# One core, a four-part edit of a decoder trunk: the last norm's column chunks, two orders of transfers, and one weight tile's place

## The chip, the cores and the metric

One core of one Trainium2 chip runs the whole program. The metric is the device time of one execution in microseconds (us), taken as the median of several runs. One execution is also profiled: its span is the time from its first to its last recorded instruction, and its own device time stands beside the span.

## The reference

The kernel computes one inference step of a decoder trunk with two layers, in float32, for a prompt of 1024 tokens and for 8 decode tokens (one for each of 8 sequences), with a model width of 1024 (D) and a feed-forward width of 2816 (D_FF). Layer A is a gated linear recurrence (HGRN2, 8 heads of 128). Layer B is sliding-window attention (window 128, 16 query heads of 64, 4 key/value heads) with sinks and a relative-position bias; its keys and values are projected once, after layer A. Each layer is followed by a SwiGLU feed-forward network, and a final RMSNorm gives the output. Cut to the lines that matter:

```python
# every sub-layer: h = h + gate(c) * F(rmsnorm(h) * (1 + scale(c)) + shift(c))
for l in range(2):
    xn = modulate(h, norm_w[l, 0], sh1, sc1)
    if l == 0:   # A: HGRN2 recurrence over chunks of 64, output gate, w_o
        mix, s_new = hgrn2_mixer(xn, w_in_a[l], w_o_a[l], gnorm_a[l], lbs[l], s0, chunk)
    else:        # B: window attention on the shared K/V; decode tokens use the caches
        q = xn @ w_q_b[0]
        att = swa_prompt(q, k_sh, v_sh, sinks, rel_bias)   # or swa_sample(q, k_buf, v_buf, ...)
        mix = att @ w_o_b[0]
    h = h + g1 * mix
    h = h + g2 * swiglu(modulate(h, norm_w[l, 1], sh2, sc2), w_ffn_in[l], w_ffn_out[l])
    if l == 0:   # shared K/V, and the caches moved on by one row
        k_sh, v_sh = split(modulate(h, kv_norm_w, sh_kv, sc_kv) @ w_kv)
        k_state = concatenate([k_buf, k_sh])[:, -WINDOW:]      # same for v
y = rms_norm(h, final_norm_w)
```

## The kernel before

**Data and products.** Activations stand transposed: 128 features on the partitions, tokens along the free axis, 1032 columns (1024 of the prompt, then 8 of decode). Every float32 product is made of three reduced-precision ones: weights and activations are split in a high and a low part, and `mm3` (lines 291 to 293) issues high x high, high x low and low x high into one accumulator. The 1032 columns are cut into equal chunks by a `Grid`: `G3` has 3 chunks of 344 columns, `G4` has 4 of 258. The decode columns are the last 8 of the last chunk (`Grid.last`).

**Weights.** The class `Stream` (object `ws`) holds the order in which weight tiles are used. A unit is loaded by the sync engine's queue (SP; lines 197, 219 and 243) into one of three `raw` buffers, cast by ScalarE (line 182) to the high part, and subtracted by GpSimd, at some places VectorE (line 185), to the low part, in one of 8 `wu` buffers. `ws.next()` hands out the unit that is used now and asks for as many units ahead as fit into `ws.look` buffers, 6 of the 8; a unit of two tiles has size 2, so three such units are ahead.

**Who orders the work.** The program is written as generators (`q_proj`, `wo_first`, `attention` and so on). `run((gen, weight), ...)` takes a step of each in turn, `queue` puts steps behind the current loop, and a `yield` ends a step. A planner then fixes the order of instructions on each engine from their readiness and their order in the program; `fix` and `keep_in_program_order` pin an instruction to its place in the program. The queues themselves run in order: a transfer that waits holds up all that stand behind it on SP.

**The four places.**
1. *Layer A's output projection.* `hgrn_proj(hh)` (line 966) makes the four input projections of head hh with `ws.next()` for each. After the last head, `wo_first` (line 1377) makes the first half of the output projection with four units of W_o, in chunks of `G4`; `wo_product` (line 1369) is one tile of 128 output features by one chunk, 12 matmuls, and `residual` (line 845) adds the gated result to the residual.
2. *The bias tiles.* `biases()` (line 1296) is called once, from the first feed-forward network (`ffn`, line 1599), between two hidden tiles (`seven_products(j)`, some 20 us each): it loads constants, makes a row of 384 biases for each of 16 heads by one matmul and one VectorE addition, writes it to DRAM (`rd`), spreads it to 128 partitions in DRAM (`gd`, 3 MB), loads the sinks and, for each of the 8 decode sequences, one sink column and two pieces of the row, and copies the two caches from DRAM to DRAM.
3. *Layer B's output projection.* Its residual comes back from DRAM (`reload_stack`, line 1425, which issues at line 658): chunk 0 before `next(second)`, chunks 1 to 3 after `next(dec)`. Each chunk is two transfers. `decode_attention` (line 1763) begins with eight transfers, in its first step: the old cache rows (line 1769, four transfers of 128 rows) and the new ones (line 1774, four short ones); its second step transposes them on TensorE (line 1789). `dec_first` runs the rest of it before the projection's last chunk.
4. *The last stage.* The second feed-forward network's last output products run over `G3` chunks and 8 tiles of features (lines 1628 to 1645) with `Final` (line 1994) as their norm. `Final.square` squares the new residual, `then(c)` sums the squares by matmuls with a vector of ones (line 2062), takes the root on VectorE (`newton`, line 542), transposes blocks of 128 tokens back (line 2021), scales the rows and writes them (lines 2040 to 2046). The chunks hold token blocks 0 and 1, 2 to 4, 5 to 7; the last block group's transposes are partly made ahead (`early`, `before_last`), and the decode tokens' rows come with the last chunk:

```python
            if c == LAST:
                dec = [self.turn(NB, lambda k: hd[:, k, :], i, (mmp, axp)[i]) for i in range(2)]
```

## Time and profile before

| | |
|---|---|
| median of 3 runs | 2501.37 us (2498.51, 2501.37, 2503.21) |
| the profiled execution's own time | 2500.0 us |
| its span | 2498.1 us |
| mean granted TensorE clock | 0.996 of full speed |
| busy share of TensorE, VectorE, ScalarE, GpSimd | 98%, 56%, 36%, 31% |
| moved by DMA | 293.43 MB, mean 117 GB/s |

The profile comes from one execution. Busy time of an engine counts its computing instructions; waits, branches and the issue of transfers are not counted. The granted clock is given as a share of full speed: 1.0 is 2.4 GHz, 0.5 is 1.2 GHz. The two rows below the time are of that one execution; the median is of others.

### The profile page before, as it was taken

To read this page: it belongs to the slowest core of one execution; us is meant where nothing else is said; L and a number is where in the kernel's file an instruction comes from. 1 tells how busy PE (TensorE), PEld (TensorE's weight loads), DVE (VectorE), ACT (ScalarE), POOL (GpSimd) and SP (SyncE) were. 2 spreads that over 40 slices of the span, in tenths; PEclk is the share of its full clock that TensorE was granted. 3 is DMA by queue.
4 is the path that set the end of the run, shared out by engine and by line. 5 is a ranking of instruction groups with operands and counts; after the bars stand their busy time and mean duration, and the time that the engine had idled before them with its cause. 6 is when DMAs were issued, how large, how long until landed. Compare 5 with 4: busy or idle time off the path is not lost.

```text
span 2498.1 us, 52373 instructions
## 1 busy us (share of the span) xinstructions
PE 2454.3 (98%) x21557; PEld 2338.0 (94%) x21557; DVE 1390.8 (56%) x3177; ACT 903.0 (36%) x2012; POOL 774.6 (31%) x560
## 2 busy tenths in 40 slices
PE   7999999999999999999999999999999999999998
PEld 5999999998889999999999998878999999999998
DVE  6444444456486554656433735576885555565436
ACT  5333333332363332333211555454643333333112
POOL 1211111111225444544432131002364444445221
PEclk9999999999999999999999999999999999999999
DMA  9465522246833224326321322523222222264101
GB/s 332 146 214 178 170 76 72 70 131 211 267 106 94 82 84 144 97 83 233 123 77 51 93 56 65 165 85 110 69 86 77 77 77 81 82 228 148 65 26 69
DMA packets 314561, 293.43 MB, mean 117 GB/s; under 512 B 28681, under 2 KB 291738, under 8 KB 314290
## 3 DMA queue, kind: packets, MB, share of 16 engines
q1 hardware_dynamic: 313920, 289.86, 35.8%
q8 instruction: 170, 2.79, 0.5%
q14 instruction: 69, 0.57, 0.1%
q10 hardware_dynamic: 402, 0.22, 0.0%
HBM read 231.27 MB, written 63.99 MB: 118 GB/s over the span
## 4 chain that ended last, share of the span: by engine, by line
PE 89%; DVE 4%; DMA 3%; issue 2%; ACT 1%; SPq 0%; POOL 0%; ACTq 0%; DVEq 0%; POOLq 0%
PE mm L291 20%; PE mm L293 19%; PE mm L292 19%; PE ax L291 6%; PE ax L292 6%; PE ax L293 6%; PE ax L470 2%; PE ax L1943 1%; PE ax L1872 1%; PE ax L1098 1%; PE ax L1929 1%; PE ax L1225 1%; PE ax L1188 1%; DMA raw<-in_w_ffn_in_dram 1%; DMA gd<-rd 1%
## 5 line engine op out<-in xcount | busy, mean ns | idle before, releaser
L185 POOL TENSOR_TENSOR wu<-raw,wu 128x512 fp32r<-128x512 f32 x460 | 628.5, 1374 | 1380.1 <-ACT wu L182 1279.4
L291 PE MATMUL mm<-c,wu 128*128 128x344 f32 (+1 forms) x2104 | 673.8, 320 | 2.8 <-ACT c L917 1.7
L293 PE MATMUL mm<-c,wu 128*128 128x344 f32 (+1 forms) x2104 | 660.6, 314 | 1.9 <-issue 1.9
L292 PE MATMUL mm<-c,wu 128*128 128x344 f32 (+1 forms) x2104 | 662.0, 315 | 0.3 <-DVE c L920 0.3
L182 ACT CAST wu<-raw 128x512 fp32r<-128x512 f32 x464 | 286.0, 620 | 665.8 <-PE mm L293 358.5
L291 PEld LDWEIGHTS mm<-c,wu 128*128 128x128 f32 x2104 | 397.4, 189 | 16.1 <-issue 9.4
L292 PEld LDWEIGHTS mm<-c,wu 128*128 128x128 f32 x2104 | 397.8, 189 | 4.2 <-issue 2.6
L293 PEld LDWEIGHTS mm<-c,wu 128*128 128x128 f32 x2104 | 397.9, 189 | 1.8 <-issue 1.8
L291 PE MATMUL mm<-xq,wu 128*128 128x258 f32 x1376 | 390.3, 284 | 2.4 <-ACT wu L182 1.0
L293 PE MATMUL mm<-xq,wu 128*128 128x258 f32 x1376 | 389.6, 283 | 1.3 <-POOL wu L185 1.3
L292 PE MATMUL mm<-xq,wu 128*128 128x258 f32 x1376 | 388.2, 282 | 1.2 <-DVE xq L838 1.2
L291 PE MATMUL ax<-xq,wu 128*128 128x258 f32 x1120 | 316.4, 282 | 0.0
L293 PE MATMUL ax<-xq,wu 128*128 128x258 f32 x1120 | 315.8, 282 | 0.0
L292 PE MATMUL ax<-xq,wu 128*128 128x258 f32 x1120 | 315.6, 282 | 0.0
L291 PEld LDWEIGHTS mm<-xq,wu 128*128 128x128 f32 x1376 | 259.6, 189 | 4.1 <-DVE c L1502 1.2
L292 PEld LDWEIGHTS mm<-xq,wu 128*128 128x128 f32 x1376 | 260.7, 189 | 1.7 <-DVE xq L838 1.7
L293 PEld LDWEIGHTS mm<-xq,wu 128*128 128x128 f32 x1376 | 259.7, 189 | 2.8 <-POOL wu L185 1.5
L845 DVE SCALAR_TENSOR_TENSOR hs<-mm,ada,hs 128x344 f32<-128x344 f32 (+3 forms) x228 | 120.7, 533 | 173.3 <-PE mm L293 164.4
L292 PEld LDWEIGHTS ax<-xq,wu 128*128 128x128 f32 x1120 | 212.1, 189 | 0.0
L291 PEld LDWEIGHTS ax<-xq,wu 128*128 128x128 f32 x1120 | 211.5, 189 | 0.0
L293 PEld LDWEIGHTS ax<-xq,wu 128*128 128x128 f32 x1120 | 211.1, 188 | 0.0
L845 DVE SCALAR_TENSOR_TENSOR c<-mm,ada,c 128x344 f32<-128x344 f32 (+1 forms) x132 | 74.8, 571 | 112.1 <-PE mm L293 111.4
(329 smaller groups left out, 3603.1 us busy)
## 6 DMA issues: line engine op xcount, KB each, us to landing
c<-in_w_ada_dram SPq DMA_DIRECT2D x96, 512.0 KB
raw<-in_w_ffn_in_dram SPq DMA_DIRECT2D x160, 256.0 KB
ff<-c SPq DMA_DIRECT2D x44, 516.0 KB
c<-ff SPq DMA_DIRECT2D x44, 516.0 KB
raw<-in_w_ffn_out_dram SPq DMA_DIRECT2D x44, 512.0 KB
raw<-in_w_in_a_dram SPq DMA_DIRECT2D x32, 512.0 KB
hs<-hs SPq DMA_DIRECT2D x16, 516.0 KB
out_dram<-c SPq DMA_DIRECT2D x16, 512.0 KB
```

Source lines behind the costliest of these rows:

```text
L182: i = act.copy(u[:, 0, :], src)
L185: j = eng.tensor_tensor(u[:, 1, :], src, u[:, 0, :], op=ALU.subtract)
L291: put(pe.matmul(ps, wh, xh, start=first, stop=False))
L292: put(pe.matmul(ps, wh, xl, start=False, stop=False))
L293: put(pe.matmul(ps, wl, xh, start=False, stop=last))
L470: pe.matmul(ada_ps[q][32 * j : 32 * j + 32, 256 * i : 256 * i + 256], cT[:, k, :], u[i][:, j, :], start=(k == 0 and i == 0), stop=(k == KT ...
L845: dve.scalar_tensor_tensor(hc, ps[:, : g.pl[c]], ada[:, gate + n, 0:1], hc, op0=ALU.mult, op1=ALU.add)
L1098: pe.matmul(ps[32 * j : 32 * j + 32, c * 32 : (c + 1) * 32], KS[:, t0 : t0 + 32], QP[:, t0 : t0 + 32], start=True, stop=True, tile_positio ...
L1188: pe.matmul(ps[:, j * P : (j + 1) * P], kt[:, s], vt[:, s], start=True, stop=True)
L1225: pe.matmul(o, attT[:, c, :], vt[:, s], start=(c == 0), stop=True)
L1872: pe.matmul(psv[hf][:, gi, s0:256], q[2 * gp + gi][r, tb * P : (tb + 1) * P], kT[a][r, (tb - 1) * P + s0 : (tb + 1) * P], start=True, stop ...
L1929: pe.transpose(ps[:, g * P : (g + 1) * P], L[:, g, sb * P : (sb + 1) * P], ident)
```

## The change

It has four parts.

1. A class `Blocks` (object `GB`) takes the place of `G3` in the last stage: its chunks are of whole token blocks, (5 to 7 with the 8 decode columns: 392 columns), (2 to 4: 384), (0 and 1: 256), in this order. The decode columns go with the first chunk instead of the last, and so do their residual, squares, scale, sums, root and output rows. Each square now lies in a temporary tile of its own size (`big`) and is added by VectorE or GpSimd in turn; the last one is summed by TensorE straight from its tile, with two blocks instead of three. `wo_product` and `residual` ask the grid for the width of a chunk.
2. `biases()` becomes a generator that is stepped once per hidden tile from the middle one on: constants; the small matmul and the addition; the row's write; the spread with the sinks and the first two of the 8 groups; three times two more groups, the last of them with nothing behind it until the next step; the cache copies. The two row pieces of each group are now pinned.
3. `reload_stack` is stepped in three: chunk 0, chunk 1, chunks 2 and 3. In layer B's projection chunk 1 now comes before `decode_attention`'s first step, which only loads the old cache rows, then come chunks 2 and 3, then its second step with the new rows. In layer A's both reloads run through as before.
4. For the last unit of the last head, `ws.look` is 4 instead of 6, so the third unit of W_o is asked for by the next `ws.next()`, the first of `wo_first`.

```diff
@@ -44,6 +44,9 @@
         self.last, self.nq = self.n - 1, w // Q
+    def width(self, c):
+        return self.w
     def all(self, c):
@@ -51,7 +54,29 @@
         return slice(self.cs[c], self.cs[c] + self.pl[c])
+class Blocks:
+    n, last = 3, 0
+    blocks = ((5, 8), (2, 5), (0, 2))
+    def __init__(self):
+        self.cs = [b0 * P for b0, _ in self.blocks]
+        self.pl = [(b1 - b0) * P for b0, b1 in self.blocks]
+        self.w = max(self.pl) + NB
+    def width(self, c):
+        return self.pl[c] + (NB if c == self.last else 0)
+    def all(self, c):
+        return slice(self.cs[c], self.cs[c] + self.width(c))
+    def prompt(self, c):
+        return slice(self.cs[c], self.cs[c] + self.pl[c])
 G3, G4 = Grid(344), Grid(258)
+GB = Blocks()
 W, NCH, LAST = G3.w, G3.n, G3.last
@@ -846,7 +871,7 @@
         if c == g.last:
-            dve.tensor_tensor(tdec[:, n, :], ps[:, g.pl[c] : g.w], ada[:, gate + n, 1:9], op=ALU.mult)
+            dve.tensor_tensor(tdec[:, n, :], ps[:, g.pl[c] : g.width(c)], ada[:, gate + n, 1:9], op=ALU.mult)
     def residual_dec(tdec):
@@ -968,7 +993,10 @@
         for i in range(4):
+            ws.look = 4 if hh == NH - 1 and i == 3 else RING - 2
             u = ws.next()
+            ws.look = RING - 2
             t = f if i == 0 else big()
@@ -1302,13 +1330,16 @@
         sp.dma_start(outs, k_outside)
+        yield
         ps = axp()
...
         gd = dp.tile([16, P, 384], F32, name="gd")
+        yield
         sp.dma_start(rd, rrow)
+        yield
         sp.dma_start(gd, bc(rd, 1, P))
@@ -1317,13 +1348,16 @@
             fix(sp.dma_start(skd[16 * b : 16 * b + 16, :], sinks_b[0].unsqueeze(1)))
-            sp.dma_start(biasd[16 * b : 16 * b + 16, 1:P], rd[:, P : 2 * P - 1])
-            sp.dma_start(biasd[16 * b : 16 * b + 16, 0:1], rd[:, 2 * P - 1 : 2 * P])
+            fix(sp.dma_start(biasd[16 * b : 16 * b + 16, 1:P], rd[:, P : 2 * P - 1]))
+            fix(sp.dma_start(biasd[16 * b : 16 * b + 16, 0:1], rd[:, 2 * P - 1 : 2 * P]))
+            if b % 2:
+                yield
         fix(sp.dma_start(ck_sample[:, 0 : WIN - 1], cache_swa_k[:, 1:WIN]))
...
             tc.keep_in_program_order(dve.tensor_scalar(t, t, -1.0, None, op0=ALU.mult))
-        return late, biasd, gd, sk, skd
+        yield
+        bs.extend((late, biasd, gd, sk, skd))
     for hh in range(NH):
@@ -1371,7 +1405,7 @@
             xh, xl = o.at(k, g, c)
-            mm3(ps[:, : g.w], wcol(u, 0, i), wcol(u, 1, i), xh, xl, k == 0, k == 3)
+            mm3(ps[:, : g.width(c)], wcol(u, 0, i), wcol(u, 1, i), xh, xl, k == 0, k == 3)
         residual(ps, c, n, gate, tdec, g)
@@ -1426,9 +1460,9 @@
         res.append(st)
-        st.move(src, [0], True)
-        yield
-        st.move(src, range(1, g.n), True)
+        for cs in ([0], [1], range(2, g.n)):
+            st.move(src, cs, True)
+            yield
     def factors(x, st):
@@ -1597,7 +1631,7 @@
         for j in range(PLAIN, NF):
-            if j == NF // 2 and aside:
+            if j >= NF // 2 and aside:
                 aside()
@@ -1630,16 +1664,18 @@
                     last.before_last()
-                wo_product(us[n // 2], o, c, n, gff, tdec, bank=anyp)
+                wo_product(us[n // 2], o, c, n, gff, tdec, last.g, anyp)
                 last.square(c, n)
...
                     last.early()
-            if c == LAST:
+            if c == last.g.last:
                 residual_dec(tdec)
                 last.square_dec()
+            if c == LAST:
                 last.scale_end()
+            if c == last.g.last:
                 last.scale_dec()
@@ -1685,7 +1721,8 @@
     bs = []
-    nkv = ffn(0, X, st, back[0], ToKV, lambda: bs.extend(biases()))
+    bias_steps = biases()
+    nkv = ffn(0, X, st, back[0], ToKV, lambda: next(bias_steps, None))
     late, biasd, gd, nsk, nskd = bs
@@ -1768,6 +1805,7 @@
                 dst.append(t)
+        yield
         for dst, c0 in ((kst, 0), (vst, 256)):
@@ -1975,10 +2013,12 @@
     next(second)
+    next(loads)
     dec = decode_attention()
...
         pass
+    next(dec)
     def dec_first(o=o):
@@ -1992,6 +2032,9 @@
     class Final(Norm):
+        def __init__(self):
+            Norm.__init__(self, GB)
         def scale(self, c, k):
@@ -2000,19 +2043,25 @@
         def scale_tile(self, c, k):
-            s = G3.prompt(c)
+            s = GB.prompt(c)
             return dve.tensor_scalar(h[k][:, s], h[k][:, s], nT[:, 40 + k : 41 + k], None, op0=ALU.mult)
...
         def square(self, c, k):
-            if c < LAST or k < KT - 1:
-                Norm.square(self, c, k)
+            s, n = GB.prompt(c), GB.pl[c]
+            dst = self.acc[k % 2][:, s]
+            if k < 2:
+                act.activation(dst, h[k][:, s], AF.Square)
+                return
+            t = big(cols=3 * P)[:, :n]
+            act.activation(t, h[k][:, s], AF.Square)
+            if c == LAST and k == KT - 1:
+                self.end = t
             else:
-                e0 = G3.prompt(c).start - 5 * P
-                act.activation(self.end[:, e0:], h[k][:, G3.prompt(c)], AF.Square)
+                eng = dve if k % 2 else pool
+                eng.tensor_tensor(dst, dst, t, op=ALU.add)
         def turn(self, parts, src, half, bank, ps=None, ks=range(4), put=lambda i: i):
@@ -2027,12 +2076,10 @@
             flush()
-            self.ahead = {(b, 0): self.block(b, 0, axp) for b in (5, 6, 7)}
-            self.end = big(cols=3 * P)
-            pool.memset(self.end[:, : G3.prompt(LAST).start - 5 * P], 0.0)
+            self.ahead = {(b, 0): self.block(b, 0, axp) for b in range(*GB.blocks[LAST])}
         def before_last(self):
-            for b in (5, 6, 7):
+            for b in range(*GB.blocks[LAST]):
                 self.ahead[b, 1] = self.block(b, 1, mmp, ks=range(2))
@@ -2047,7 +2094,7 @@
             yield LAG
-            b0, b1 = ((0, 2), (2, 5), (5, 8))[c]
+            b0, b1 = GB.blocks[c]
             n = b1 - b0
@@ -2060,25 +2107,23 @@
                 fix(pe.matmul(dst, src, ones[:, 0:1], start=(i == 0), stop=(i == len(sums) - 1)))
+            if c == GB.last:
+                psd = axp()
+                for i, a in enumerate(self.acc):
+                    pe.matmul(psd[:NB, 0:1], a[:, T:TOK], ones[:, 0:1], start=(i == 0), stop=(i == 1))
             if c == LAST:
-                psd = mmp()
-                for i, a in enumerate(self.acc):
-                    fix(pe.matmul(psd[:NB, 0:1], a[:, T:TOK], ones[:, 0:1], start=(i == 0), stop=(i == 1)))
-            if c == LAST:
-                for b in (5, 6, 7):
+                for b in range(b0, b1):
                     self.block(b, 1, None, ps=self.ahead[b, 1], ks=range(2, 4), put=fix)
...
             y = small([P, 12], "ny")
-            if c == LAST:
+            if c == GB.last:
                 dve.memset(ms[:, n : n + 1], 1.0)
...
             dve.tensor_scalar(ms[:, :n], ps[:, :n], 1.0 / D, EPS, op0=ALU.mult, op1=ALU.add)
-            w = n + (c == LAST)
+            w = n + (c == GB.last)
             newton(y[:, :w], ms[:, :w], w, P, "n")
-            if c == LAST:
-                dec = [self.turn(NB, lambda k: hd[:, k, :], i, (mmp, axp)[i]) for i in range(2)]
             yield 1
@@ -2088,7 +2133,8 @@
                 yield 1
-            if c == LAST:
+            if c == GB.last:
+                dec = [self.turn(NB, lambda k: hd[:, k, :], i, axp) for i in range(2)]
                 self.rows(NB, dec, y[:NB, n : n + 1], y_sample.rearrange("b s f -> (b s) f"))
```

## Rows read from the trace of the kernel before

**Rows 1.** The page: busy time, share of the span and instructions of each engine, and TensorE's granted clock in 40 equal slices of the span (9 is 90% or more).

```profile
PE 2454.3 (98%) x21557; PEld 2338.0 (94%) x21557; DVE 1390.8 (56%) x3177; ACT 903.0 (36%) x2012; POOL 774.6 (31%) x560
...
PEclk9999999999999999999999999999999999999999
```

**Rows 2.** Windows of 100 us. Columns: window, its length, busy us (instructions) of PE, PEld, DVE, ACT and POOL, granted clock, DMA share, GB/s.

```profile
500.00:600.00 100.00, 93.54 (x1382) 85.41 (x1380) 58.11 (x138) 31.90 (x101) 10.91 (x8) 0.98 0.58 182
900.00:1000.00 100.00, 97.71 (x805) 96.53 (x804) 52.59 (x103) 28.00 (x57) 43.37 (x32) 1.00 0.37 119
1600.00:1700.00 100.00, 99.16 (x749) 78.62 (x747) 68.31 (x285) 52.39 (x183) 2.58 (x2) 0.98 0.41 129
1900.00:2000.00 100.00, 100.00 (x837) 100.00 (x836) 55.36 (x110) 32.06 (x65) 44.88 (x35) 1.00 0.25 80
2300.00:2400.00 100.00, 100.00 (x638) 100.00 (x637) 42.50 (x78) 16.06 (x23) 31.94 (x21) 1.00 0.20 65
2400.00:2500.00 100.00, 89.07 (x600) 88.15 (x598) 51.34 (x139) 21.11 (x40) 16.89 (x16) 0.97 0.13 49
```

**Rows 3.** Timeline of SP's queue around the bias tiles. Columns: start, length of the group, queue, line, operation, out<-in, count.

```profile
909.37 3.85 SPq L243 DMA_DIRECT2D raw<-in_w_ffn_in_dram  x4
...
936.09 1.47 SPq L1311 DMA_DIRECT2D rd<-c  x1
939.44 0.60 SPq L1312 DMA_DIRECT2D gd<-rd  x1
...
947.75 0.98 SPq L1321 DMA_DIRECT2D late<-rd  x1
952.47 0.32 SPq L1319 DMA_DIRECT2D skd<-in_sinks_b_dram  x1
...
963.01 1.30 SPq L243 DMA_DIRECT2D raw<-in_w_ffn_in_dram  x2
```

**Rows 4.** Timeline of TensorE, some of the instructions that waited. In brackets: the idle time before, and what ended it.

```profile
551.27 0.95 PE L1267 MATMUL ax<-ident,c 128*128 128x128 f32 x4 [2.12 <-DVE c L1254]
...
978.41 0.39 PE L291 MATMUL mm<-xq,wu 128*128 128x258 f32 x1 [0.98 <-ACT wu L182]
...
980.22 0.39 PE L293 MATMUL mm<-xq,wu 128*128 128x258 f32 x1 [1.31 <-POOL wu L185]
...
1627.23 1.06 PE L1789 MATMUL ax<-late,c 128*128 128x8 f32 x8 [0.31 <-ACT c L1785]
...
1629.88 0.42 PE L291 MATMUL mm<-c,wu 128*128 128x258 f32 x1 [0.36 <-DVE hs L845]
```

**Rows 5.** Timeline of SP's queue around layer B's first output projection.

```profile
1611.87 2.45 SPq L1769 DMA_DIRECT2D c<-in_cache_swa_k_dram  x2
1614.38 3.51 SPq L1769 DMA_DIRECT2D c<-in_cache_swa_v_dram  x2
1620.64 4.54 SPq L1774 DMA_DIRECT2D c<-nd  x4
1625.23 4.09 SPq L658 DMA_DIRECT2D hs<-hsc  x6
```

**Rows 6.** The waits of VectorE on transfers between 1600 and 1660: total, times, longest.

```profile
DVE hs L845 <- DMA hs<-hsc: 8.1, 1, 8.1
```

**Rows 7.** Short windows with columns as in rows 2: five us behind the wait at 551, four us from 1630, and one us of the end.

```profile
551.00:556.00 5.00, 4.73 (x27) 4.73 (x28) 3.61 (x9) 0.00 (x0) 0.00 (x0) 0.66 0.99 328
...
1630.00:1634.00 4.00, 4.00 (x21) 4.00 (x22) 2.30 (x11) 0.66 (x4) 0.00 (x0) 0.57 1.09 351
...
2492.00:2493.00 1.00, 0.00 (x0) 0.00 (x0) 1.00 (x2) 0.72 (x2) 0.00 (x0) 1.00 1.01 410
```

**Rows 8.** Timeline of GpSimd and VectorE around the third and fourth unit of W_o.

```profile
528.71 1.29 POOL L185 TENSOR_TENSOR wu<-raw,wu 128x512 fp32r<-128x512 f32 x1 [10.65 <-ACT wu L182]
...
546.13 0.16 DVE L550 TENSOR_TENSOR ot<-ot,oms 128x10 f32<-128x10 f32 x1
...
547.49 2.98 POOL L185 TENSOR_TENSOR wu<-raw,wu 128x512 fp32r<-128x512 f32 x2 [15.29 <-ACT wu L182]
...
547.62 1.28 DVE L550 TENSOR_TENSOR ot<-ot,oms 128x10 f32<-128x10 f32 x1
```

**Rows 9.** Timeline of the end of the program, engines in the order of time.

```profile
2465.64 1.40 PE L2062 MATMUL ax<-ones,c 128*128 128x1 f32 x12
...
2484.78 0.32 PE L293 MATMUL mm<-c,wu 128*128 128x344 f32 x1
...
2485.74 0.48 ACT L2015 ACTIVATE c<-c 128x336 f32<-128x336 f32 x1 [2.17 <-DVE c L845]
...
2487.14 0.16 DVE L2077 TENSOR_SCALAR nms<-ax 128x3 f32<-128x3 f32 x1 [1.10 <-PE ax L2062]
...
2488.09 0.17 DVE L542 TENSOR_SCALAR nt<-nms 128x4 int32<-128x4 int32 x1
...
2488.53 0.60 PE L2021 MATMUL mm<-ident,hd 128*8 128x128 f32 x4
...
2490.34 2.07 DVE L2043 TENSOR_SCALAR c<-mm,ny 128x512 f32<-128x512 f32 x3
...
2491.16 2.85 SPq L2046 DMA_DIRECT2D out_dram<-c  x4
```

## The prediction

> **What bounds the kernel now.** Read the page first: TensorE is busy 98% of the span, no other engine more than 56%, and its clock is at the upper level (2.4 GHz) in nearly every slice [rows 1]. So only two things can shorten the run: less TensorE work, or one of the few places where TensorE stands still or runs at the lower level. The windows of 100 us say where those are [rows 2]: between 1900 and 2000 TensorE is busy for all 100.00 us, but 500 to 600 lacks 6.46 us, 900 to 1000 lacks 2.29, 1600 to 1700 lacks 0.84, and 2400 to 2500 holds the end of the program. The timeline names the instruction that came late at each [rows 4], and for the ones that waited for data the sync engine's queue (SP) says why [rows 3, 5]. All four places lie next to something that the change edits. The sum is made against the profiled execution's own 2500.0 us (span 2498.1), which is 1.4 below the median of the three runs shown.
>
> **Part 1, the biases in steps: -2.3 us.** Today one call issues everything between two hidden tiles. SP sends the bias row at 936.09, when VectorE has made it, and waits for it to land before the 3072 KB spread at 939.44. It issues seven small transfers, the last at 947.75, then stands until 952.47 for the spread, and comes to the next weights only at 963.01 [rows 3]. Weights usually leave every 20 us (909.37, and 929.54 by the same beat), so the next load, due at 949.5, is 13.5 late. It is also slow, since 2 MB of cache copies go out just ahead of it: the new tile is first multiplied at 978.41, after 0.98 us of waiting, and its other half at 980.22, after 1.31 [rows 4]. Together 2.29, the whole deficit of that window.
>
> After the change these instructions lie in eight hidden tiles, some 20 us each. No instruction is removed; the row's write is asked for a tile after its addition, the spread a tile after the write, and the cache copies four tiles after the spread. What is late next: the spread still blocks SP once, because its step issues the spread, the sinks and two groups of three, eight transfers, and today the ninth (952.47) waited for the spread to land. That costs SP 13.0 us (939.44 to 952.47) instead of the 26.9 from 936.09 to 963.01. Today 13.5 us of lateness plus a slow landing cost 2.3 of TensorE. A block of 13.0 that may start anywhere in a 20 us beat, without the cache copies behind it, should leave nothing. Bounds: nothing gained if the steps end up side by side again, 2.3 if the waits go. I take 2.3. The addition on VectorE and one small matmul move by a tile and cost what they cost.
>
> **Part 2, the residual before the decode caches: -2.4 us.** In layer B's first output projection, SP issues the four cache transfers from 1611.87 to 1617.89, then waits for them to land before the four short new rows (1620.64 to 1625.18), and only then sends the residual's remaining chunks, six transfers from 1625.23 [rows 5]. VectorE needs the second chunk from about 1621 and waits 8.1 us for it [rows 6]. TensorE goes on until its accumulators are full: 0.31 and 0.36 us of waiting [rows 4], and a little over a microsecond later it runs at 1.2 GHz. The four us from 1630 to 1634 show a mean level of 0.57, so 4 x 0.43 = 1.7 us of work are lost [rows 7]. Total 0.67 + 1.7 = 2.4.
>
> The change puts the second chunk's two transfers ahead of the caches and the other four ahead of the new rows. Each moves 516 KB; at the 351 GB/s of that window it takes 1.5 us [rows 7]. The second chunk should then be issued by about 1613 and land by about 1617, four us before VectorE asks. Cover for that: the queue and attention loads ahead of it are unchanged. What is late next are the new rows, behind six more transfers, so up to 9.0 us later; who waits for them are the decode transposes on TensorE. If these stand as far back in its queue, nothing is lost. Bounds: a gain of 2.4, a loss of 8.3 (below). I take the gain, being the nearer: today the transposes found their data without a wait for a transfer in these rows.
>
> **Part 3, the last chunks: -0.7 us.** First the products. 837 matmuls of 258 columns fill 100 us, 638 of 344 columns too [rows 2]: 0.1195 and 0.1567 us each, hence about 0.43 ns a column and 8 ns beside. 392, 384 and 256 columns are then 0.1775, 0.1741 and 0.1186, together 0.4702, against three times 0.1567 = 0.4702. The 288 products cost the same.
>
> The end is shorter. Now the last product starts at 2484.78, the square of its residual 0.96 later (0.48 long), the mean is taken at 2487.14, the root begins at 2488.09 and the rows are scaled from 2490.34 [rows 9]. With 256 columns instead of 336 I estimate 0.1 off the residual and 0.1 off the square, and four passes of the last sums instead of six, at 1.40/12 = 0.12 each, 0.2 off. The 0.95 between mean and root goes to some 0.2, because the decode part that stands there is done two chunks earlier. Together 1.2. Then two outputs instead of four are issued: 0.66 us each in the row of 2.85 for four, so 1.3 less, and 1.05 instead of 1.6 MB at 410 GB/s [rows 7] give the same 1.3. Sum 2.5, between 2.0 and 3.2 according to how far issue and data overlap.
>
> Against it, work that now hides behind that end comes in front of it, where TensorE is the bound: the eight decode transposes (0.60 for four to the end of the last: 0.9 for eight), the two decode sums (0.24), four more passes of sums (0.5) and two more transposes (0.2): 1.8, from 1.3 to 2.5. Net -0.7, between -1.9 and +0.5. The squares' temporaries move to the large slots; VectorE's load in this window (51 of 100 us) covers that.
>
> **Part 4, the third tile: 0.** Its two subtractions on GpSimd run from 528.71 [rows 8], and the tile isn't multiplied before TensorE's wait at 551.27 [rows 4]. Asked for later it loses rank and no work: one 512 KB transfer, two casts, two subtractions. Cover is the 20 us between. If that went, the transfer costs 512 KB at 351 GB/s, 1.5 us. The place nearby is delicate: TensorE waits 2.12 us at 551.27 for VectorE [rows 4] and the five us from 551 to 556 have a mean level of 0.66, another 5 x 0.34 = 1.7 [rows 7]: 3.8 could be won if VectorE came earlier. VectorE was late because a short operation took 1.28 us at 547.62 instead of 0.16, while GpSimd subtracted the fourth tile [rows 8]. The Trainium skill (SBUF — State Buffer, section "SBUF: two separate sides") says that VectorE with two SBUF inputs and GpSimd share a port pair that one holds for a whole instruction. By that rule the third tile's two subtractions, if they slid to this place, would add two such blocks, 2 x 1.1 = 2.2 us; the row agrees with the rule, and the sum would be -3.2. Bounds without it, from these rows: -3.8 to +2.2.
>
> **Sum.** -2.3 - 2.4 - 0.7 + 0 = -5.4: 2494.6 for the profiled time, 2496.0 on the scale of the median. I name 2495.
>
> **Rivals.**
> (a) The decode transposes take the place of the wait removed. For: six transfers of 1.5 us stand ahead of the new rows, and TensorE's order is fixed before the run. Against: the same edit moves the transposes behind in program order. Full price 9.0 waiting plus 1.7 at the lower level, less today's 2.4: +8.3, with parts 1 and 3 2505.3, slower. It decides from a wait of some 9 us on; a wait of 1 to 3 us only eats the gain: 2496 to 2499. Chance 0.08 full, 0.10 small.
> (b) Part 2 or part 1 gives nothing, because the planner puts the transfers out in much the old order: 2497.0. For: it has freedom on SP. Against: three of the bias transfers a group are now pinned. Chance 0.10.
> (c) The third tile's subtractions slide into VectorE's chain, two more blocks of 1.28 - 0.16 = 1.1 [rows 8], +2.2: 2496.8. For: they rank lower than before; against: their slot is free at 528. Chance 0.08.
> (d) The chain at 551 comes earlier and its wait and the lower level go: -3.8, 2490.8. For: the ranks there change. Against: no operation of that chain is edited. Chance 0.14.
> (e) The change does nothing that counts: 2499.8 or so. Chance 0.04.
> My forecast, 2494.6, has 0.46.
>
> **Numbers.** What a measurement of this kernel can tell from no change is about 0.2%, 5 us, so faster begins at a gain of 5.0. The forecast's gain is 5.4, and its own range, 2492 to 2497, is a gain of 3 to 8: some three quarters of its chance, 0.35, lie beyond 5.0. With (d) that is 0.49. Its other quarter, (b), (c), (e) and the small case of (a) give 0.43; slower 0.08. The range 2489 to 2501 holds (d) at one end and reaches to the unchanged time at the other, and leaves out only the full case of (a).
>
> **What would show it.** Part 1: TensorE's windows 900 to 1000 full, SP never more than about 13 us away from the weights. Part 2: no wait of VectorE for the residual near 1621, no stretch at the lower level near 1631, no TensorE wait at the decode transposes. Part 3: from the last product to the end of the span 10.8 us instead of 13.3. Part 4: the wait of 2.1 near 551 and its lower level still there. It is wrong if a new wait of over 2 us stands before TensorE anywhere.

## The result and the profile after

The changed kernel is slower by a little: 2505.02 us (median of 18 runs, 2500.04 to 2508.84) against 2499.86 for the kernel before (18 runs beside them, 2498.12 to 2503.21). The ratio is 1.0020, with a 95% interval of 1.0014 to 1.0027, or +5.2 us (3.5 to 6.7). The forecast was 2495, faster; the time also lies above the range. The profiled execution took 2504.92 us, span 2503.1, so the two profiles differ by 5.0 us of span, about as the medians do.

The page of after, first line, as in [rows 1]: the busy time of TensorE has grown by 5.7 us over practically the same matmuls, so on balance the loss is not idle time (what the new waits add, other places give back) but work at the lower clock, and work moved in front of the end (part 3).

```profile
PE 2460.0 (98%) x21555; PEld 2342.2 (94%) x21555; DVE 1388.6 (55%) x3177; ACT 902.2 (36%) x2012; POOL 776.1 (31%) x559
```

Windows of 100 us of after, columns as in [rows 2]. Between 900 and 1000 the deficit is 1.82 where it was 2.29, and 1100 to 1200, full before, now lacks 1.82 as well. Between 1600 and 1700 nothing was won, and the clock is lower than before.

```profile
900.00:1000.00 100.00, 98.18 (x806) 96.99 (x805) 50.97 (x105) 28.54 (x58) 36.48 (x28) 0.99 0.31 97
1100.00:1200.00 100.00, 98.18 (x729) 97.77 (x728) 60.92 (x110) 35.61 (x59) 52.44 (x33) 0.98 0.58 201
1600.00:1700.00 100.00, 99.08 (x743) 81.20 (x740) 61.17 (x254) 46.95 (x165) 2.60 (x2) 0.97 0.42 129
2400.00:2500.00 100.00, 94.99 (x631) 93.36 (x629) 52.62 (x143) 22.38 (x42) 19.71 (x17) 0.99 0.11 43
```

The window from 1100 in before:

```profile
1100.00:1200.00 100.00, 100.00 (x753) 100.00 (x753) 59.10 (x111) 36.96 (x59) 54.42 (x34) 1.00 0.55 198
```

To find where the time came from, each product of the program was paired with the same product in the other trace and their start times subtracted. After minus before, in us:

| stretch of the program | the difference changes by | stands then at |
|---|---|---|
| up to 540 | +0.9 | +0.9 |
| the place at 551 | -1.8 | -0.9 |
| 900 to 980 (before's wait gone) | -2.8 | -3.7 |
| about 1000 (new wait) | +3.8 | +0.1 |
| about 1125 (new wait) | +3.9 | +4.0 |
| 1130 to 1600 | -0.2 | +3.8 |
| 1600 to 1700 (layer B's first output projection) | +2.1 | +5.9 |
| 1700 to 2240, then 2241 | +0.3, -1.2 | +5.0 |
| 2240 to the last product | +2.9 | +7.9 |
| behind the last product | -2.9 | +5.0 |

The -1.2 at 2241 belongs to no part of the change: before's profile has two short waits there (0.36 and 0.42 us) that the profiles of part2 and part4 (below), which edit nothing near, don't have either.

The two new waits, in TensorE's timeline of after. They have the form of the two of before at 978 and 980 [rows 4].

```profile
997.69 0.39 PE L316 MATMUL mm<-xq,wu 128*128 128x258 f32 x1 [0.98 <-ACT wu L207]
...
999.04 0.58 PE L318 MATMUL mm<-xq,wu 128*128 128x258 f32 x1 [0.84 <-POOL wu L210]
...
1122.52 0.39 PE L316 MATMUL mm<-xq,wu 128*128 128x258 f32 x1 [0.98 <-ACT wu L207]
...
1123.87 0.39 PE L318 MATMUL mm<-xq,wu 128*128 128x258 f32 x1 [0.84 <-POOL wu L210]
```

Short windows of after: the stretch between the transfers and the first new wait, then one window behind each new wait, and the group of decode matmuls in layer B.

```profile
979.00:994.00 15.00, 15.00 (x127) 15.00 (x126) 6.30 (x16) 1.26 (x3) 0.00 (x0) 1.00 0.01 2
...
1000.00:1002.00 2.00, 2.00 (x11) 2.00 (x10) 1.75 (x2) 0.00 (x0) 2.00 (x3) 0.50 0.64 192
...
1126.00:1128.00 2.00, 2.00 (x11) 2.00 (x11) 2.00 (x3) 1.11 (x3) 2.00 (x3) 0.50 0.00 0
...
1644.00:1648.00 4.00, 4.00 (x26) 3.30 (x26) 2.34 (x15) 2.99 (x15) 0.00 (x0) 0.93 0.01 2
1648.00:1652.00 4.00, 4.00 (x14) 3.14 (x14) 2.19 (x14) 1.08 (x6) 0.00 (x0) 0.50 0.00 0
1652.00:1656.00 4.00, 4.00 (x24) 3.44 (x22) 0.85 (x4) 2.15 (x7) 0.00 (x0) 0.71 0.00 0
```

In each new place TensorE stands for 0.98 + 0.84 = 1.82 us and then runs for a while at 1.2 GHz. Around the first place the two-us windows from 998 show 0.73, 0.50 and 0.92; the first of them contains the second half of the wait, and 2 x (0.27 + 0.50 + 0.08) = 1.7 us of work are lost. With 1.82 that is 3.5 of the 3.8. The second is the same to 0.1. In layer B no wait comes before the fall: 4 x (0.07 + 0.50 + 0.29) = 3.4 us are lost while TensorE is busy throughout. The Trainium skill (TensorE: Matmul & The Clock Gate, "Part 1: The HAM clock gate") says that the gate has two levels and none between. The traces agree: windows that lie inside a fall show 0.50, and only those that hold an edge show something else.

### The profile page after: what moved, and what is told of

It reads as the page before. It is cut to its first block, busy times and chain, and to the rows that moved or that the text cites. A ratio compares the mean times of both kernels' runs of the same rounds, so it can differ in the third digit from the quotient of the medians.

```text
span 2503.1 us, 52357 instructions
## 1 busy us (share of the span) xinstructions
PE 2460.0 (98%) x21555; PEld 2342.2 (94%) x21555; DVE 1388.6 (55%) x3177; ACT 902.2 (36%) x2012; POOL 776.1 (31%) x559
## 5 line engine op out<-in xcount | busy, mean ns | idle before, releaser
L316 PE MATMUL mm<-c,wu 128*128 128x344 f32 (+2 forms) x2104 | 672.9, 320 | 1.7 <-ACT c L942 1.7
L317 PE MATMUL mm<-c,wu 128*128 128x344 f32 (+2 forms) x2104 | 661.7, 315 | 0.3 <-DVE c L945 0.3
L318 PE MATMUL mm<-c,wu 128*128 128x344 f32 (+2 forms) x2104 | 660.3, 314 | 1.4 <-issue 1.4
L316 PEld LDWEIGHTS mm<-c,wu 128*128 128x128 f32 x2104 | 396.7, 189 | 13.5 <-issue 8.5
L318 PEld LDWEIGHTS mm<-c,wu 128*128 128x128 f32 x2104 | 397.1, 189 | 2.1 <-issue 2.1
L316 PE MATMUL mm<-xq,wu 128*128 128x258 f32 x1376 | 391.4, 285 | 3.3 <-ACT wu L207 2.0
L318 PE MATMUL mm<-xq,wu 128*128 128x258 f32 x1376 | 390.0, 283 | 1.7 <-POOL wu L210 1.7
L316 PE MATMUL ax<-xq,wu 128*128 128x258 f32 x1120 | 317.4, 283 | 0.0
L318 PE MATMUL ax<-xq,wu 128*128 128x258 f32 x1120 | 316.4, 283 | 0.0
L316 PEld LDWEIGHTS mm<-xq,wu 128*128 128x128 f32 x1376 | 260.5, 189 | 5.2 <-ACT wu L207 2.4
L318 PEld LDWEIGHTS mm<-xq,wu 128*128 128x128 f32 x1376 | 260.5, 189 | 3.4 <-POOL wu L210 2.1
L318 PEld LDWEIGHTS ax<-xq,wu 128*128 128x128 f32 x1120 | 212.3, 190 | 0.0
L316 PEld LDWEIGHTS ax<-xq,wu 128*128 128x128 f32 x1120 | 212.0, 189 | 0.0
L870 DVE SCALAR_TENSOR_TENSOR c<-mm,ada,c 128x344 f32<-128x344 f32 (+3 forms) x132 | 74.7, 570 | 113.0 <-PE mm L318 111.4
```

Source lines behind the costliest of these rows:

```text
L316: put(pe.matmul(ps, wh, xh, start=first, stop=False))
L317: put(pe.matmul(ps, wh, xl, start=False, stop=False))
L318: put(pe.matmul(ps, wl, xh, start=False, stop=last))
L870: dve.scalar_tensor_tensor(hc, ps[:, : g.pl[c]], ada[:, gate + n, 0:1], hc, op0=ALU.mult, op1=ALU.add)
```

## The experiments

Each run was timed beside the kernel before, on the same chip. The difference is to the median of those runs of before; its interval is worked out from the ratio's.

| run | median us | ratio, 95% interval | difference us (interval) |
|---|---|---|---|
| part1 | 2502.89 | 1.0011, 1.0002 to 1.0019 | +2.6 (0.5 to 4.8) |
| part2 | 2503.58 | 1.0014, 1.0005 to 1.0023 | +3.3 (1.3 to 5.8) |
| part3 | 2500.09 | 0.9998, 0.9989 to 1.0007 | -0.2 (-2.8 to 1.8) |
| part4 | 2499.17 | 0.9993, 0.9985 to 1.0002 | -1.1 (-3.8 to 0.5) |
| part1_poolq | 2496.95 | 0.9991, 0.9982 to 1.0000 | -2.8 (-4.5 to 0) |
| pieces | 2508.03 | 1.0032, 1.0019 to 1.0044 | +8.3 (4.7 to 11) |
| chunk1_first | 2498.46 | 0.9995, 0.9986 to 1.0004 | -1.3 (-3.5 to 1.0) |
| combo | 2498.89 | 0.9997, 0.9988 to 1.0006 | -0.8 (-3.0 to 1.5) |
| part1_pinned | 2501.67 | 1.0011, 1.0001 to 1.0020 | +2.5 (0.2 to 5.0) |
| before_poolq | 2504.16 | 1.0021, 1.0012 to 1.0029 | +5.0 (3.0 to 7.2) |
| mended | 2495.39 | 0.9982, 0.9973 to 0.9991 | -3.7 (-6.7 to -2.2) |

### One part at a time

Four kernels, each the kernel before with one part of the change: **part1** the biases in steps, **part2** the residual's order, **part3** the last chunks, **part4** the weight tile asked for later.

> The kernel before with only the biases in steps. Theory O (the planned order): it fixes its order as if the weights behind each large transfer came a tile late, so after the spread, and again after the cache copies, one hidden tile's conversions stand behind the tile before, TensorE waits about 2.2 us at each of the two places and may run at 1.2 GHz for some us after each; against one such wait of 2.3 us in the kernel before. That gives +2 to +6 us, about +4.8 as read from the aligned traces. Theory P (the prediction's part 1): SP is held up only for the landing of the spread, the wait of before goes, -2.3 us.

> The kernel before with only the residual's chunks ahead of the caches and the new rows. Theory O: the wait of VectorE goes, but the decode transposes and scores come in one dense group of small matmuls, TensorE's clock falls there without a wait before it; +2 us as read from the aligned traces. Theory P: -2.4 us, and no lower level near there.

> The kernel before with only the last stage's chunks of 392, 384 and 256. From the aligned traces: the part ahead of the last product grows by 2.9 us and the part behind it shrinks by 2.9, so 0, or -1 if two short waits near 2241 that the changed kernel doesn't have go by this part. Theory P: -0.7 us (1.8 in front, 2.5 behind).

> The kernel before with only the third unit of W_o asked for later. From the aligned traces: the wait of 2.12 us at 551 becomes 1.1 and the stretch at 1.2 GHz behind it goes, and some 0.8 come back at 560 to 600: -1.8 us. Theory P: 0.

Measured: +2.6, +3.3, -0.2 and -1.1, in sum +4.6, near the +5.2 of the whole. The loss is in parts 1 and 2, and neither needs the other. Part 1's profile has the two new waits (0.98 and 0.84 us at each of two places), part 2's the fall of the clock at 1648. Parts 3 and 4 can't be told from nothing.

### Part 1: late data, or a fixed order?

SP's queue in after, columns as in [rows 3]. The spread (L1343) leaves alone, and SP then stands until 974.77 for the hidden store (`ff`, the write of a finished hidden tile to DRAM); only two of the four weight transfers follow, and the store after them.

```profile
959.82 0.60 SPq L1343 DMA_DIRECT2D gd<-rd  x1
974.77 0.33 SPq L1606 DMA_DIRECT2D ff<-c  x1
975.19 1.34 SPq L268 DMA_DIRECT2D raw<-in_w_ffn_in_dram  x2
994.80 0.34 SPq L1606 DMA_DIRECT2D ff<-c  x1
```

So far this looks like the forecast's story with a worse ending. But the first of the short windows above says that from 979 to 994 nothing is under way (DMA share 0.01): the two weight tiles of 975.19 had landed, and VectorE, ScalarE and GpSimd had room. ScalarE's timeline in after:

```profile
990.03 0.42 ACT L1601 ACTIVATE c<-c 128x258 f32<-128x258 f32 x1 [9.63 <-DVE c L1600]
...
995.32 0.38 ACT L1586 COPY c<-mm 128x258 f32<-128x258 f32 x1 [3.43 <-PE mm L318]
996.74 0.38 ACT L1586 COPY c<-ax 128x258 f32<-128x258 f32 x1 [1.05 <-PE ax L318]
997.01 1.14 ACT L207 CAST wu<-raw 128x512 fp32r<-128x512 f32 x2
```

The casts of the tile come at 997.01, some 18 us after its data, behind two copies of the coming tile's first product, which TensorE releases only after the end of the tile at work. ScalarE sat idle for 9.63 and 3.43 us meanwhile. What it does first is fixed before the run. In that fixed order six casts of the coming tile normally stand ahead of the end of the tile at work; here, and again behind the cache copies at 1083, none does. In before this is so at one place only, at 978. There the data is late as well, VectorE waits 1.92 us for a weight transfer, so that before's trace alone doesn't part the two causes:

```profile
977.55 0.69 DVE L254 TENSOR_TENSOR raw<-raw,raw 128x512 f32<-128x512 f32 x1 [1.92 <-DMA raw<-in_w_ffn_in_dram]
```

The order looks as if the planner had reckoned with weights that come a tile late behind a large transfer; what it reckoned with is not in the traces, only the order that came of it. Splitting one group of transfers into two places made two such tiles.

**part1_poolq** issues the spread and the cache copies on GpSimd's queue, otherwise as part1:

```diff
-        sp.dma_start(gd, bc(rd, 1, P))
+        pool.dma_start(gd, bc(rd, 1, P))
...
-        fix(sp.dma_start(ck_sample[:, 0 : WIN - 1], cache_swa_k[:, 1:WIN]))
-        fix(sp.dma_start(cv_sample[:, 0 : WIN - 1], cache_swa_v[:, 1:WIN]))
+        fix(pool.dma_start(ck_sample[:, 0 : WIN - 1], cache_swa_k[:, 1:WIN]))
+        fix(pool.dma_start(cv_sample[:, 0 : WIN - 1], cache_swa_v[:, 1:WIN]))
```

> The biases in steps, as in part1, with the spread and the two cache copies issued by GpSimd's queue instead of SP's, so that SP never stands for them; the planned order of VectorE keeps its two late places (35 and 31 instructions between the conversions of two tiles instead of 18). Theory O (planned order): both waits of some 2.2 us stay, +2 to +3 us against the kernel before, like part1. Theory Q (SP is held up by the large transfers): the waits go, -2.3.

Measured -2.8, the figure of theory Q, and no wait of TensorE between 900 and 1200. But SP is not free in it, as theory Q has it. Its queue in part1_poolq, then VectorE's first sum for the weights, and two lines of ScalarE:

```profile
957.21 0.36 SPq L1313 DMA_DIRECT2D rd<-c  x1
975.61 0.33 SPq L1578 DMA_DIRECT2D ff<-c  x1
983.57 15.69 SPq L243 DMA_DIRECT2D raw<-in_w_ffn_in_dram  x8
```

```profile
987.29 1.76 DVE L254 TENSOR_TENSOR raw<-raw,raw 128x512 f32<-128x512 f32 x1 [2.60 <-DMA raw<-in_w_ffn_in_dram]
```

```profile
986.51 0.62 ACT L182 CAST wu<-raw 128x512 fp32r<-128x512 f32 x1 [3.30 <-DMA raw<-in_w_ffn_in_dram]
...
998.21 0.37 ACT L1558 COPY c<-mm 128x258 f32<-128x258 f32 x1
```

SP stands for the store as long as in after with no large transfer on its queue, and the weights leave 8 us later than there (983.57 against 975.19; some 7 when the two programs are aligned). VectorE waits 2.60 for them and ScalarE 3.30. Yet TensorE doesn't wait at all: in this kernel's fixed order casts of the coming tile stand ahead of the two copies, from 986.51 on at the first place (copies at 998.21) and from 1080.88 on at the second (copies at 1100.33). Later data and no wait, against earlier data and a wait: it is the order, not the lateness, that costs. The order isn't the one that the expectation took for granted: the queue was the edit, and the planner's order changed with it.

**pieces** cuts the spread and both cache copies into eight and puts one of each into every step (`gd[hs2]`, `ck_sample[b]`, `cv_sample[b]` on SP, then `yield`).

> The biases in steps, with the spread and the cache copies cut into eight pieces, one piece of each a tile (some 0.6 MB, against 1 MB of weights a tile). No transfer is large any more, but the planned order falls back one tile at the first piece (50 instructions on VectorE between two conversions instead of 18) and does not catch up until the last tiles. Theory O: TensorE waits some 2.2 us at every tile from there on, five to seven times, less the one wait of before: +8 to +14 us. Theory Q: no transfer holds up the weights, no wait, -2.3.

Measured +8.3, in five runs. The number of waits was a miss: there is one pair, at 1040 (0.98 and 0.84), where again no cast stands ahead of the two copies (1038.01 and 1039.38), and afterwards none while the hidden tiles last. From there on two casts of the coming tile stand ahead of its copies each time (1056.96, the copy at 1060.48), fewer than usual and enough. The bill comes where the order of work changes, at the first output products:

```profile
1161.12 0.42 PE L291 MATMUL mm<-c,wu 128*128 128x344 f32 x1 [0.51 <-ACT wu L182]
...
1163.81 0.65 PE L292 MATMUL mm<-c,wu 128*128 128x344 f32 x1 [2.27 <-DVE c L1592]
```

Between 1160 and 1170 TensorE is busy for 6.3 us of 10, and its granted clock is 0.79 and then 0.52 over five us each; by paired starts the place costs 6.8 of the 8.3.

**part1_pinned** is part1 with the loads, casts and first sums pinned to program order from the middle tile on, all transfers still on SP:

```diff
-        if len(ws.done) <= 4:
+        if len(ws.done) <= 4 or pin[0]:
...
+            pin[0] = not l and j >= NF // 2
```

> The biases in steps as in part1, all transfers on SP as there; only the order is changed: from the middle tile on, the weights' loads, casts and first sums of the first feed-forward network are pinned to their place in the program, so that no tile's sums stand behind the ends of two tiles on VectorE (in part1 two tiles' do, in the kernel before one, in part1_poolq none). Theory O (the planned order of the conversions): both waits of part1 go, about -2.3 us against the kernel before, less what pinned sums that wait for their weights hold up on VectorE. Theory Q (the transfers hold up the weights on SP): the waits stay, +2.6.

Measured +2.5, unresolved against part1, and theory Q's figure rather than theory O's. One wait of the two is gone, the one behind the cache copies; the first is as it was. ScalarE's timeline of part1_pinned shows the same idle engine and the same two copies ahead of the casts:

```profile
997.33 0.38 ACT L1570 COPY c<-ax 128x258 f32<-128x258 f32 x1 [1.05 <-PE ax L305]
997.60 1.14 ACT L184 CAST wu<-raw 128x512 fp32r<-128x512 f32 x2
```

At the first place the casts came out as late as without the pins, at the second one of them came ahead. So the edit made the intended order at one place of two, and the wait is gone at that one: the waits come and go one by one with the order. The loads were pinned too, though, and left earlier at the second place than in part1 (1083.20 against 1100.89), so this run doesn't part order and data there by itself. What does part them is when the data landed: in part1 by about 1105, some 18 us ahead of the cast at 1122.68 that TensorE waited for; in part1_pinned just in time, a cast at 1096.75 waited 0.54 us for it, and TensorE for nothing.

**before_poolq** is the kernel before, all in one call, with the same three lines on GpSimd's queue as above.

> The kernel before, biases in one call, with only the spread and the cache copies issued by GpSimd's queue. In the planned order no tile's first sums stand behind two tiles' ends. Theory O: the one wait of 2.3 us goes without any steps, -2.3 to -2.8 us. Theory Q agrees here, since SP is free of the large transfers too; a time like that of the kernel before would speak against both.

Measured +5.0, against both theories: the queue alone is no gain, though the wait at 978 is gone as theory O had it. VectorE's wait and one of the small transfers on SP in before_poolq:

```profile
963.57 0.15 DVE L1325 TENSOR_SCALAR skd<-skd 128x1 f32<-128x1 f32 x1 [12.34 <-DMA skd<-in_sinks_b_dram]
```

```profile
953.84 2.71 SPq L1320 DMA_DIRECT2D late<-rd  x1
```

The sinks and rows share the 16 DMA engines with the spread and both copies, which now move all at once. Small transfers that take 0.42 us each at 940 take up to 2.71 at 954, VectorE's negation of the sinks, pinned to its place, stands 12.34 us behind the last, and TensorE waits 3.4 us for the work queued behind it and 0.8 once more; between 960 and 970 its granted clock is 0.76. By paired starts that costs 7.7 us, and the wait at 978 that is gone gives 2.8 back. The Trainium skill (DMA: Bandwidth & Descriptors, "Issuing engines are not separate DMA queues") says that transfers from different engines interleave on the same 16 DMA engines, so that a second queue saves only issue time; this run agrees. That part1_poolq gains by the second queue all the same is the work of its other order, as shown above. In steps the spread and the copies are four tiles apart, and part1_poolq has nothing of it. So the steps are worth having, with the second queue and not without.

By their times alone these runs don't decide for the order: of theory O's figures, those of part1 and pieces came, and those of part1_poolq, part1_pinned and before_poolq did not. What decides is in the traces: in after and part1 the data had landed some 18 us before, ScalarE was idle and the casts stood behind the two copies at each place where TensorE waits 0.98 and 0.84; in part1_poolq, and at the second place of part1_pinned, casts stand ahead of the copies, the data comes late or just in time, and there is no such wait.

### Part 2: the decode transposes

SP's queue in after, to be read beside [rows 5]. The new rows (L1812) leave at 1630.50, 9.9 us later than before; 3.8 of these are the delay that the whole program has by then.

```profile
1615.59 2.98 SPq L683 DMA_DIRECT2D hs<-hsc  x2
1618.62 3.20 SPq L1806 DMA_DIRECT2D c<-in_cache_swa_k_dram  x2
1621.91 3.09 SPq L1806 DMA_DIRECT2D c<-in_cache_swa_v_dram  x2
1625.10 5.35 SPq L683 DMA_DIRECT2D hs<-hsc  x4
1630.50 3.02 SPq L1812 DMA_DIRECT2D c<-nd  x4
```

The waits of [rows 4] at 1627 and 1629 and VectorE's wait of [rows 6] are gone, as forecast. In their place TensorE's order, which follows the transfers, has the decode work later and closer together: between 1643.21 and 1650.65 there is no product of the output projection (L316 to L318) at all, only groups like these of after's timeline.

```profile
1646.06 1.13 PE L1910 MATMUL ax<-c,c 64*128 64x256 f32 x4
1647.12 1.59 PE L1827 MATMUL ax<-late,c 128*128 128x8 f32 x8
1648.64 2.07 PE L1910 MATMUL ax<-c,c 64*128 64x256 f32 x4
```

The clock falls inside this group, with no wait ahead of it; from 1647 the same forms take longer (1.59 for the eight that took 1.06 at 1643.85, 2.07 for the four that took 1.13).

**chunk1_first** keeps the good half: the second chunk ahead of the old cache rows, the other two behind the new rows, as before.

```diff
-        st.move(src, [0], True)
-        yield
-        st.move(src, range(1, g.n), True)
+        for cs in ([0], [1], range(2, g.n)):
+            st.move(src, cs, True)
+            yield
...
+    next(loads)
```

> The kernel before with only chunk 1 of the residual ahead of the old cache rows; the new rows come before chunks 2 and 3, as before, so that the decode transposes are planned apart, as before. Theory D (the dense group of decode matmuls makes part 2 slower): VectorE's wait of 8 us goes, and the decode groups keep 20 to 50 lines of weight products between them: -0.7 if the lower level near 1630 comes from the 8-column matmuls alone, -2.4 if it comes from the two short waits. Rival: the residual in front delays the caches and the new rows, and the time is that of part2, +3.

Measured -1.3, unresolved from nothing, but 4.6 below part2, each against its own runs of before. Its 100 us are full, and the clock does not fall:

```profile
1600.00:1700.00 100.00, 99.97 (x772) 80.57 (x768) 64.92 (x270) 49.97 (x176) 2.58 (x2) 1.00 0.41 129
...
1648.00:1652.00 4.00, 4.00 (x32) 3.43 (x31) 3.51 (x18) 3.55 (x13) 0.00 (x0) 1.00 0.00 0
```

So part 2's loss hangs on chunks 2 and 3 standing ahead of the new rows. TensorE hardly waits for anything in either kernel; what differs is its order.

How much was there to win at 1630? Seven of the other profiled kernels have the order of before here (part1, part3, part4, part1_poolq, part1_pinned, pieces, before_poolq). TensorE lacks 0.3 to 1.4 us between 1624 and 1640 in them, 0.67 in before; but the fall of the clock in [rows 7] is in before's profile alone. In part3, for one:

```profile
1630.00:1634.00 4.00, 3.97 (x35) 3.61 (x36) 2.70 (x10) 0.83 (x2) 0.00 (x0) 1.00 1.09 360
```

### What is worth keeping

**combo** is chunk1_first with parts 3 and 4, the biases in one call. **mended** is the changed kernel with the three transfers on GpSimd's queue and the new rows ahead of chunks 2 and 3 again.

> chunk1_first with part 3 and part 4, and the biases in one call as in the kernel before. If the parts add up: -0.7 or -2.4 from the residual, -0.2 from part 3, -1.1 from part 4: -2 to -3.7 us against the kernel before, at the edge of what can be told from it.

> The changed kernel with two edits: the spread and the cache copies on GpSimd's queue, and the new rows ahead of chunks 2 and 3 of the residual again (chunk 1 stays ahead of the caches). If the two costs found are all that made the change slower, the parts add up: -2.8 from part1_poolq, -1.3 to -2.7 from chunk1_first, -0.2 and -1.1 from parts 3 and 4: -4 to -7 us against the kernel before.

combo: -0.8, less than the 2 to 3.7 expected, and unresolved. mended: -3.7 (2.2 to 6.7), just short of the 4 to 7 expected, faster than before, and some 9 below after, each against its own runs of before. Its windows of TensorE from 900 to 1000 and 1600 to 1700 are full but for 0.02 us. What it keeps is the wait at 551 (2.1); one of 0.73 at 1176, at the first output products, is in its profile and not in before's. The sum of the separate runs part1_poolq, chunk1_first, part3 and part4 would be -5.4; the interval holds that.

## Why the prediction was wrong

**Part 1 (-2.3 forecast, +2.6 measured).** The step that failed is "a block of 13.0 that may start anywhere in a 20 us beat ... should leave nothing". The block was sized about right: SP stands away from the weights from 959.82 to 975.19, 15.4 us. But it isn't the spread that blocks SP, as forecast: with the spread on another queue, in part1_poolq, SP stands for the hidden store as long. And it was weighed as lateness of data against a beat, when the wait is set by the places of the casts in ScalarE's fixed order. By that, moving the transfers apart makes two waits of one. That the wait is ended by ScalarE and not by a transfer stood in [rows 4] ("ACT wu") and was read past. No rival had this; the last sentence of the prediction, a new wait of over 2 us anywhere, is nearly what came: 1.82 idle, twice, and 1.7 at the lower clock behind each in the profiled execution. In part1's own profile the same two waits left the clock at 1.00, as here from 996 to 1004:

```profile
996.00:1004.00 8.00, 6.18 (x49) 5.76 (x49) 3.62 (x5) 2.82 (x6) 4.03 (x4) 1.00 0.26 88
```

So the part costs one wait more than before and now and then a fall more. By paired starts each pair of waits costs 2.4 us in part1 and before's pair 2.8, somewhat more than the idle time that is shown. Two pairs for one make some +2 without a fall, within the interval of part1's +2.6.

**Part 2 (-2.4 forecast, +3.3 measured).** Two steps failed. First the size: 1.7 of the 2.4 were a fall of the clock that is in one of eight profiles of this order, so some 0.7 was there to win. (Of the 0.67, 0.31 was a wait for a copy of ScalarE [rows 4], which the forecast put down to full accumulators.) Second, "if these stand as far back in its queue, nothing is lost". They did stand back, and there was hardly a wait (0.9 us in three kinds between 1670 and 1680), so rival (a) is not what happened either. They stood back in one dense group, and that cost 3.4 at the lower clock. 3.4 + 0.9 less the 0.7 of idle time that went is +3.6 against an execution of before that doesn't lose the clock there, beside +3.3 measured.

**Part 3 (-0.7 forecast, -0.2 measured).** Within its bounds, in part by luck: both of its terms came out larger than named, and one paid for the other. The end of after, beside [rows 9]:

```profile
2492.67 0.28 PE L318 MATMUL mm<-c,wu 128*128 128x256 f32 x1
...
2493.55 0.42 ACT L2059 ACTIVATE c<-c 128x256 f32<-128x256 f32 x1 [1.56 <-DVE c L870]
...
2494.67 0.16 DVE L2124 TENSOR_SCALAR nms<-ax 128x2 f32<-128x2 f32 x1 [0.31 <-PE ax L2109]
2494.86 0.17 DVE L567 TENSOR_SCALAR nt<-nms 128x2 int32<-128x2 int32 x1
...
2497.10 1.41 DVE L2090 TENSOR_SCALAR c<-mm,ny 128x512 f32<-128x512 f32 x2
...
2497.91 0.99 SPq L2093 DMA_DIRECT2D out_dram<-c  x2
```

From the last product to the scaling it is 4.43 where it was 5.56: 1.1 saved, 1.2 forecast, and mean to root fell to 0.19 as said. From the first of these output transfers to the end of the span it is 5.2 where it was 6.9: 1.7 saved, 1.3 forecast. In all 2.9 against 2.5, or 10.4 from the last product to the end where 10.8 was to show it. But what moved in front costs 2.9 too, where 1.8 was forecast and 2.5 was the bound. TensorE does not wait there, so it is work and not a stall; which of the moved matmuls are dearer than priced wasn't separated.

**Part 4 (0 forecast, -1.1 measured).** Within what can't be told from nothing. Alone, the part keeps the wait of 2.1 at 551 and the lower level behind it. In after's profile the wait is 1.1, and the clock stays up. GpSimd and, behind it, VectorE of after at this place:

```profile
548.08 1.65 POOL L210 TENSOR_TENSOR wu<-raw,wu 128x512 fp32r<-128x512 f32 x1 [15.02 <-ACT wu L207]
550.61 1.28 POOL L210 TENSOR_TENSOR wu<-raw,wu 128x512 fp32r<-128x512 f32 x1 [0.88 <-ACT wu L207]
```

```profile
548.49 1.27 DVE L575 TENSOR_TENSOR ot<-ot,oms 128x10 f32<-128x10 f32 x1
```

One short operation of VectorE still takes 1.27, as in [rows 8], but the second subtraction waited 0.88 for ScalarE and came after VectorE's chain instead of into it. All other profiled kernels, mended among them, have the wait of 2.1. So rival (d) came halfway in this profile, and no run shows that an edit brings it. What the place is worth stays open. After's profile gains 1.8 us there. But three others (part1_poolq, part1_pinned, chunk1_first) keep the upper level behind the wait of 2.1, and from 540 to 600 they stand at +0.1, -0.3 and +1.1 against before, two of them because the clock falls at 576 instead.

**The sum.** -5.4 was forecast and +5.2 came: +4.9 of the 10.6 are part 1, +5.7 part 2, +0.5 part 3 and -1.1 part 4, by the separate runs, which leaves 0.6 within their uncertainty. The numbers for queues and durations were mostly good; what failed was to take the order on the engines as given while the transfers moved.

## What to carry to other kernels

Where the order of every engine is planned ahead, price a moved transfer by the order that results on the engines that convert its neighbours' data, and not only by when bytes arrive: an idle engine beside landed data, with the late instruction behind one that waits for the tile's end, is how such a loss looks. Two costly transfers at one place may cost one wait, and apart two, if the planned order falls behind at each. Don't book as a gain a stretch at the lower clock that one execution shows: look for it in a second profile first, and whether the clock falls a little later there instead.

## What the runs showed of the hardware

The clock's fall behind a wait is a matter of the execution. Mean granted clock of the same stretch in the thirteen profiles:

```
stretch                              at 1.00                            lower
545-560, wait of 2.1                 part1_poolq, part1_pinned,         .89 in the nine others
                                     chunk1_first
574-584, wait of 1.4 to 3.0          the nine others                    .83 in part1, part4, part1_poolq; .66 in chunk1_first
975-1010, one wait pair, 978-982     before, part4                      .95 in part2, part3, combo, chunk1_first
975-1010, one wait pair, 997-1001    part1, part1_pinned                .95 in after
1624-1640, order of before           the seven kernels named above      .89 in before
1405-1430, wait of 2.0               before, pieces, after              .93 in the ten others
1640-1660, dense decode group        -                                  .83 in after, part2
```

(After's own wait at 551 is 1.1 long and is left out of the first line.) A fall that stays out at one wait may come at the next: of the three profiles that keep the upper level at 551, two lose it at 576. And before's profile, unlucky at 1630, is one of the three without a fall at 1405 to 1430. The 18 runs of after, which spread over 8.8 us, go with the clock: the six with the highest mean clock (0.995) have a median of 2502.6, the five with the lowest (0.992 and 0.993) 2507.0. And TensorE can lose the upper clock while it is never idle: in the dense decode group, in both kernels that have it, and in none of the others. That the order brings the group and the fall is shown; what in the group makes the clock fall is not.
